# Two-block transformer on one core: the second block's memory keys and values as split passes in pieces, and the test for crowded experts one step earlier

## The chip, the cores and the metric

The kernel runs on one core of a Trainium2 chip. The metric is device time in microseconds from the start of the kernel to its end, median of three executions. One further execution was taken by the hardware profiler, and the rows below come from that one.

## The reference, cut to what matters

Two blocks work on one sequence of 256 tokens with 1024 channels, in fp32. The first block has a convolution layer, a dense feed-forward layer, a layer of sliding-window attention and a layer of eight experts, of which each token takes two. The second block has two hybrid layers, each with a feed-forward layer behind it. Each hybrid layer also attends to a memory of 256 rows, and the keys and values of that memory do not depend on the tokens:

```
def memory_attn(q, mem_n, w_mkv):
    kv = (mem_n @ w_mkv).reshape(B, M, 2, N_HEADS_M, HEAD_DIM)
    s = jnp.einsum('bshd,bmhd->bhsm', q, kv[:, :, 0])
    p = jax.nn.softmax(s, axis=-1)
    o = jnp.einsum('bhsm,bmhd->bshd', p, kv[:, :, 1])
...
def second_block(x, mem, ...):
    for l in range(DEPTH):                     # two layers
        # keys and values of layer l: rms_norm(mem, g_mem[l]) @ w_mkv[l], 1024 x 512
        x = hybrid_layer(x, mem, ...)
    return rms_norm_2(x, norm_final)
...
def moe_swiglu(h, router, we_gate, we_up, we_down):
    top_v, top_i = lax.top_k(h @ router, 2)
    gates = one_hot(top_i) * softmax(top_v)    # 256 x 8
    for e in range(N_EXPERTS):
        out = out + gates[..., e:e + 1] * swiglu(h, we_gate[e], we_up[e], we_down[e])
```

## The kernel before

**The order of the work.** A class `Recorder` takes all operations first and then issues them. `flush` hands what was recorded to `issue`, a list scheduler with its own costs and free places for the buffers: it sets the order of each engine's instructions, and each engine executes its own list in that order. All recorded operations carry the line of the one call in `issue` that emits them, L694 in the rows before. `flush` is called at the test described below and at the end, so no operation moves across the test.

**Weights.** A weight tile is 128 x 1024 fp32 (512 KB) and is loaded on SP's queue into one of 28 `large` buffers. The dense layers use *split passes*: `load` makes two halves of a tile, a high half on ACT and the rest on DVE (by subtraction), in two further `large` buffers; `feed` does the same for the activations; `mm3` issues three matmuls of the type fp32r, high x high, high x low, low x high. In the experts and, before the change, in the second block's memory keys and values the matmuls are plain fp32; a plain fp32 matmul stands in the trace as two records.

**Experts.** `experts` runs 32 steps, four for each expert (31 is the last one's fourth). Step n projects up to 96 gathered tokens (`proj(n)`, 16 tiles of `e_in`, in each expert's fourth step 8), applies the activation (`act`), and then does the down projection of the step before (`down(n-1)`, 8 tiles of `e_down`, in a fourth step 4). When an expert is complete, `scatter` adds its result to the tokens: an evacuation of PSUM on ACT and DVE and matmuls on PE. `prepare(0)` gathers the tokens of the first two experts.

**The test.** `route` also yields the count `most` of the fullest expert. `moe` reads it and passes over the code for more than 96 and more than 192 tokens, which does not run with these inputs:

```
self.nc.flush()
most = self.tc.nc.values_load(self.most[0:1, 0:1], min_val=0, max_val=S)
with ExitStack() as inner:
    for base in range(CAP, S, CAP):
        inner.enter_context(self.tc.If(most > base))
        self.scatter(*self.experts(float(base)))
        self.nc.flush(aside=True)
self.scatter(back, y)
self.nc.release(held)
self.fill(200)
```

All 32 steps stand ahead of the test, the scatter of the last expert behind it. Each engine executes its own branch (line 1327 before).

**The memory.** `mem_second(l)` loads the memory (`mem2T`, four tiles of 256 KB), computes the root mean square (`rstd`, `bcast`), scales it by the gains on ACT, loads `c_mk` and `c_mv` (two tiles each) and makes keys and values, 16 plain fp32 matmuls each. `MEM_AT = 2, 200` puts layer 0 behind `prepare(0)` of the first expert and layer 1 behind the last scatter. `AHEAD = 1` loads and splits the first two tiles of `c_qk`, the first hybrid layer's query and key weights, ahead of the test.

## Time and profile before

| | us |
|---|---|
| median of 3 executions | 2179.4 (2177.43 to 2180.08) |
| the profiled execution | 2182.62 |
| its span, first to last instruction | 2180.8 |
| mean granted TensorE clock | 0.992 |
| PE busy in it | 2141.2 (98%) |
| DVE busy | 965.8 (44%) |
| ACT busy | 734.0 (34%) |

The profiled execution takes 1.8 us more than its span, and 3.2 us more than the median. The page has the busy time of each engine (PE matmuls, PEld weight loads, DVE, ACT, POOL); *windows* give the same for a stretch of time, with the granted clock and the load on the DMA engines; the *timeline* gives the operations in order of time with the idle time before them and what ended it.

### The profile page before, as it was taken

What the parts mean: (1) busy time and instruction counts of PE and PEld (TensorE: products, weight loads), DVE (VectorE), ACT (ScalarE), POOL (GpSimd) and SP (SyncE); (2) the same over time, 40 slices, a digit from 0 to 9 for tenths busy, and PEclk for the clock granted to TensorE, in tenths of its full rate; (3) what the DMA queues carried; (4) which work ended last, traced back from release to release, by engine and by line L of the source; (5) the groups of instructions that cost most, each with busy time, mean ns of one, the idle gap of its engine ahead of it and who ended that gap; (6) DMA issues with size and microseconds to landing.
All of it is one profiled execution on the core that took longest, in us unless ns stands there. A gap on an engine that the chain in (4) does not pass through costs nothing. (4 is left out here: it accounts for less than half of the span.)

```text
span 2180.8 us, 57477 instructions
## 1 busy us (share of the span) xinstructions
PE 2141.2 (98%) x25496; PEld 1688.3 (77%) x25496; DVE 965.8 (44%) x2079; ACT 734.0 (34%) x1315; POOL 0.2 (0%) x4
## 2 busy tenths in 40 slices
PE   8999999999999999999999999899999999999998
PEld 8799997866565656656665656688999998899997
DVE  8975659510112011110302021666675566668553
ACT  8564547310101010010101010555554454655442
POOL 0000000000000000000000000000000000000000
PEclk9999999999999999999999999899999999999998
DMA  7445555489999999999899996653456555345550
GB/s 258 144 147 193 194 192 186 165 315 408 376 365 375 394 398 347 401 367 403 345 395 368 403 368 258 234 177 113 154 174 195 192 174 188 117 132 199 193 182 27
DMA packets 156209, 556.74 MB, mean 255 GB/s; under 512 B 17456, under 2 KB 20144, under 8 KB 155952
## 3 DMA queue, kind: packets, MB, share of 16 engines
q1 hardware_dynamic: 155952, 552.98, 69.3%
q8 instruction: 202, 3.31, 0.6%
q14 instruction: 55, 0.45, 0.1%
HBM read 551.87 MB, written 1.05 MB: 254 GB/s over the span
## 5 line engine op out<-in xcount | busy, mean ns | idle before, releaser
L694 PE MATMUL bank<-large,gen 128*32 128x256 f32 (+2 forms) x16896 | 1061.0, 380 | 0.0
L694 PE MATMUL bank<-gen,large 128*128 128x256 f32 x7468 | 943.3, 287 | 11.8 <-ACT large L694 8.1
L694 PEld LDWEIGHTS bank<-large,gen 128*32 128x32 f32 (+1 forms) x16896 | 656.7, 114 | 376.2 <-issue 6.1
L694 PEld LDWEIGHTS bank<-gen,large 128*128 128x128 f32 x7468 | 915.0, 190 | 29.8 <-issue 9.9
L694 DVE TENSOR_TENSOR large<-large,large 128x1024 fp32r<-128x1024 f32 (+1 forms) x356 | 429.6, 1210 | 129.4 <-PE bank L694 92.5
L694 ACT ACTIVATE gen<-bank 32x256 fp32r<-32x256 f32 (+7 forms) x322 | 124.2, 395 | 925.7 <-PE bank L694 897.8
L694 ACT ACTIVATE large<-large 128x1024 fp32r<-128x1024 f32 (+1 forms) x356 | 364.5, 1045 | 208.8 <-PE bank L694 120.6
L694 DVE SCALAR_TENSOR_TENSOR gen<-bank,small,gen 128x256 f32<-128x256 f32 (+2 forms) x100 | 44.3, 447 | 686.1 <-ACT gen L694 686.1
L694 ACT ACTIVATE gen<-gen 128x512 f32<-128x512 f32 (+3 forms) x149 | 89.6, 614 | 176.6 <-DVE gen L694 175.5
L694 DVE TENSOR_TENSOR gen<-bank,gen 32x256 fp32r<-32x256 f32 (+2 forms) x172 | 85.6, 505 | 138.9 <-ACT gen L694 73.4
L694 PE MATMUL bank<-gen,gen 128*128 128x192 f32 (+5 forms) x672 | 109.3, 341 | 11.8 <-ACT gen L694 7.3
L694 PEld LDWEIGHTS bank<-gen,gen 128*64 128x64 f32 (+3 forms) x672 | 68.3, 175 | 49.4 <-DVE gen L694 17.7
L694 DVE TENSOR_TENSOR gen<-gen,gen 128x512 f32<-128x512 f32 (+3 forms) x129 | 81.1, 637 | 50.2 <-ACT gen L694 48.4
L694 PE MATMUL bank<-ct,gen 128*128 128x128 f32 (+2 forms) x370 | 63.3, 275 | 7.1 <-DVE gen L694 6.8
L694 PEld LDWEIGHTS bank<-ct,gen 128*128 128x128 f32 (+1 forms) x370 | 45.2, 158 | 24.8 <-issue 13.2
L694 ACT ACTIVATE gen<-bank,small 128x256 f32<-128x256 f32 (+2 forms) x75 | 41.0, 569 | 50.5 <-PE bank L694 40.2
L694 DVE TENSOR_TENSOR xT<-xT,bank 128x512 f32<-128x512 f32 x64 | 43.6, 686 | 25.8 <-PE bank L694 24.8
L694 DVE SCALAR_TENSOR_TENSOR gen<-bank,gen 128x256 f32<-128x256 f32 (+1 forms) x66 | 25.4, 428 | 55.1 <-PE bank L694 54.5
L694 DVE SCALAR_TENSOR_TENSOR gen<-gen,pt,gen 128x256 f32<-128x256 f32 x108 | 43.3, 488 | 1.7 <-ACT gen L694 1.7
L694 DVE STREAM_TRANSPOSE gen<-gen 128x256 f32<-128x256 f32 (+1 forms) x96 | 38.7, 408 | 2.8
L694 ACT ACTIVATE gen<-gen,small 128x128 f32<-128x128 f32 x72 | 32.0, 448 | 17.8 <-DVE small L694 17.8
L694 DVE COPY small<-bank 32x1 f32<-32x1 f32 (+1 forms) x97 | 14.8, 152 | 46.6 <-ACT gen L694 44.9
(55 smaller groups left out, 374.2 us busy)
## 6 DMA issues: line engine op xcount, KB each, us to landing
large<-e_in SPq DMA_DIRECT2D x448, 512.0 KB, 6.9
large<-e_down SPq DMA_DIRECT2D x224, 512.0 KB, 6.8
large<-c_up SPq DMA_DIRECT2D x64, 512.0 KB, 4.4
large<-c_dn SPq DMA_DIRECT2D x64, 512.0 KB, 4.7
large<-c_g SPq DMA_DIRECT2D x48, 512.0 KB, 3.9
large<-c_qk SPq DMA_DIRECT2D x24, 512.0 KB, 5.9
large<-cv_gate SPq DMA_DIRECT2D x22, 512.0 KB, 4.5
large<-cv_up SPq DMA_DIRECT2D x22, 512.0 KB, 4.6
```

Source lines behind the costliest of these rows:

```text
L694: op.fn(*[real(x) for x in op.args], **{k: real(x) for k, x in op.kw.items()})
```

## The change

`mem_second` becomes a generator `memories` with four pieces: keys and values of layer 0, then of layer 1. The memory is loaded and its root mean square taken once and held. The matmuls become split passes (`load`, `feed`, `ws`, `n256`). Two pieces are taken inside the sliding-window attention (`other` of `attend` takes one behind each of the first two pairs of heads), one behind `prepare(0)`, one behind the test. `experts` becomes a generator as well and stops ahead of its last step, so that the test now stands ahead of step 31: its 8 tiles of `e_in`, 12 tiles of `e_down`, and the scatter come behind it. The loading ahead (`AHEAD`) is gone. Operations are emitted at L698 of the changed file, the test stands at its L1329.

```diff
 class Recorder
                     if key.start is None:
                         key.start = self.total
-                    key.last = self.total
+                    if key.last is None or key.last < 1 << 60:
+                        key.last = self.total
...
     def release(self, aps):
         for ap in aps:
+            ap.tile.last = self.total
             self.drop(ap.tile, 0.0)
...
     def flush(self, aside=False):
         before = dict(self.free)
+        places = {p: list(p.free) for c in self.kinds.values() for p in c.places}
...
-                    p.free = [v if v is None else min(v, top) for v in p.free]
+                    p.free = places[p]
...
 def swa_layer
-        self.attend(gs, False, ot[:6], sink=lambda g: self.P("sinks", order[g]))
+        self.later = self.memories()
+        self.attend(gs, False, ot[:6], sink=lambda g: self.P("sinks", order[g]), other=islice(self.later, 2))
...
 def moe
-        back, y = self.experts()
-        self.ahead = [self.load(self.a["c0_qk"][0, u]) for u in range(AHEAD)]
-        held = [t for j in self.xn for p in j for t in p] + [self.pos, self.gate, back, y[0], y[2]]
-        self.nc.hold(held)
-        self.nc.hold([t for w in self.ahead for p in w for t in p])
-        self.nc.flush()
+        work = self.experts()
+        held = [t for j in self.xn for p in j for t in p] + [self.pos, self.gate] + next(work)
+        nc.hold(held)
+        nc.flush()
...
-        self.scatter(back, y)
-        self.nc.release(held)
-        self.fill(200)
+        for _ in work:
+            pass
+        nc.release(held)
+        next(self.later)
...
 def experts
         prepare(0)
         if not base:
-            self.fill(2)
+            next(self.later)
         for n, s in enumerate(steps):
-            if not base:
-                self.fill(100 + n)
+            if n == len(steps) - 1 - LAST:
+                e = s[0]
+                yield G[e] + list(B[e]) + [t for k in T for t in T[k]] + [Y[e][0], Y[e][2]]
             act(s, proj(s))
...
-        return down(steps[-1])
+        self.scatter(*down(steps[-1]))
...
-    def mem_second(self, l):
+    def memories(self):
         mT = [self.t([128, 2, S], F32, f"m2T{k}") for k in range(4)]
         self.early(mT, a["mem2T"])
         rc = self.rstd(mT)
         rb = self.bcast(rc)
-        for k in range(KT):
-            x = mT[k // 2][:, k % 2]
-            nc.scalar.activation(x, x, AF.Copy, scale=self.P("memn_g", l * 8 + k))
...
+        nc.hold(mT + [rc, rb])
+        for l in range(2):
+            f = self.feed(mT, "memn_g", l * 8)
+            nc.hold([t for p in f for t in p])
+            kT = self.t([128, 2, S], F32, "m2k")
+            w = self.load(a[f"c{l}_mk"][0])
+            p = self.mm()
+            self.ws(p, w, f)
...
+            yield
+            v = self.t([128, 2, 256], F32, "m2v")
+            w = self.load(a[f"c{l}_mv"])
+            p = self.mm()
+            self.n256(p, f, w)
...
+            yield
...
 def hybrid
-                if self.ahead:
-                    w = self.ahead.pop(0)
-                    self.nat(ps, f, w, 4 * u)
-                    nc.release([t for p in w for t in p])
-                    continue
                 w = self.load(a[f"c{l}_qk"][c, u])
```

**SP's queue at the test.** Before, the list of loads from the last one of the experts over the branch to the first weights of the hybrid layer (`gen` and `large` are buffers, the name behind the arrow is the array in memory; `[waits ...]` are the semaphores that the load waits for on SP):

```order
L694 DMA large_37265<-e_down 128x1024 [waits DMAHW0_49,PE_49]
L1327 UNCONDITIONAL_BRANCH [waits DMAHW0_49,DMAHW1_49,DMAHW2_49,DMAHW3_49,DMAHW4_49,DMAHW5_49,DMAHW6_49,DMAHW7_49] x2
L694 DMA gen_37517<-mem2T 128x512 [waits DVE_49,DMAHW1_49,PE_49,Activation_49]
L694 DMA gen_37523<-mem2T 128x512 [waits DMAHW2_49]
L694 DMA large_37557<-c_mk 128x1024 [waits DMAHW5_49]
L694 DMA large_37587<-c_mv 128x1024 [waits DMAHW7_49,DMAHW0_49]
L694 DMA large_37608<-c_qk 128x1024 [waits DMAHW1_49]
L694 DMA gen_37638<-masks 128x384 [waits DMAHW3_49]
L694 DMA large_37657<-c_qk 128x1024 [waits DMAHW5_49]
```

After the change, the same place of SP's queue:

```order
L698 DMA large_37095<-e_down 128x1024 [waits DMAHW4_49,PE_49]
L1329 UNCONDITIONAL_BRANCH [waits DMAHW0_49,DMAHW1_49,DMAHW2_49,DMAHW3_49,DMAHW4_49,DMAHW5_49,DMAHW6_49,DMAHW7_49] x2
L698 DMA large_37388<-e_in 128x1024 [waits DMAHW3_49,DMAHW2_49,DMAHW4_49,DMAHW1_49,DMAHW5_49,DMAHW0_49,DMAHW6_49,DVE_49,DMAHW7_49,PE_49,Activation_49]
L698 DMA large_37390<-e_in 128x1024 [waits DMAHW4_49,DMAHW2_49,DMAHW7_49,DMAHW0_49,PE_49]
L698 DMA large_37404<-e_down 128x1024 [waits DMAHW5_49]
L698 DMA gen_37428<-masks 128x384 [waits DMAHW1_49]
L698 DMA large_37646<-c_mv 128x1024 [waits DMAHW5_49]
L698 DMA large_37652<-c_mv 128x1024 [waits DMAHW6_49]
L698 DMA large_37658<-c_qk 128x1024 [waits DMAHW7_49]
L698 DMA large_37664<-c_qk 128x1024 [waits DMAHW0_49,PE_49]
L698 DMA large_37710<-c_qk 128x1024 [waits DMAHW2_49,DVE_49]
L698 DMA large_37715<-c_qk 128x1024 [waits DMAHW7_49,DMAHW3_49,DVE_49]
```

Between the branch and the first weights of the hybrid layer there stood the memory, its keys' and its values' weights; now 20 expert tiles (8 of `e_in`, 12 of `e_down`) and the 4 masks stand ahead of `c_mv`, and `c_qk` follows it.

**ACT at the test.** Before, ACT's list from its branch on (`bank` is PSUM; `pt` the table of gains):

```order
L1327 UNCONDITIONAL_BRANCH [waits Activation_49] x2
L694 ACTIVATE gen_37515<-bank_15117 32x256 [waits DVE_49,PE_49,Activation_49]
L694 ACTIVATE gen_37515<-bank_15131 32x256
L694 ACTIVATE gen_37526<-bank_15117 32x256 [waits DVE_49]
L694 ACTIVATE gen_37548<-bank_15131 32x256
L694 ACTIVATE gen_37563<-gen_37517 128x512 [waits DMAHW1_49,PE_49]
L694 ACTIVATE gen_37517<-gen_37517,pt 128x256 [waits Activation_49]
```

After the change (`large_37648<-large_37646` is the high half of a weight tile, so it stands behind that tile's load in SP's list above):

```order
L1329 UNCONDITIONAL_BRANCH [waits Activation_49] x2
L698 ACTIVATE gen_37529<-bank_37434 128x128 [waits PE_49]
L698 ACTIVATE gen_37536<-bank_37439 128x128 [waits DVE_49,PE_49,Activation_49]
L698 ACTIVATE gen_37544<-bank_37444 128x128 [waits PE_49,Activation_49]
L698 ACTIVATE large_37648<-large_37646 128x1024 [waits DMAHW4_49,DMAHW5_49,DMAHW3_49,DMAHW6_49,DMAHW2_49,DMAHW7_49,DMAHW1_49,DMAHW0_49]
L698 ACTIVATE large_37654<-large_37652 128x1024 [waits DMAHW4_49,DMAHW3_49,DMAHW6_49,DMAHW2_49,DMAHW7_49,DMAHW1_49,DMAHW0_49]
L698 ACTIVATE large_37660<-large_37658 128x1024 [waits DMAHW7_49,DMAHW4_49,DMAHW2_49]
L698 ACTIVATE large_37684<-large_37682 128x1024 [waits DMAHW4_49,DMAHW3_49,PE_49]
L698 ACTIVATE large_37719<-large_37710 128x1024 [waits DMAHW6_49,PE_49]
L698 ACTIVATE gen_37760<-bank_15298 32x256 [waits PE_49]
L698 ACTIVATE gen_37760<-bank_15312 32x256 [waits PE_49]
```

Before, the evacuations of the last scatter (`gen<-bank 32x256`, twelve) came first behind the branch, then the memory's squares and gains. Now three evacuations of step 31's projection come first, then ten weight splits (two of `c_mv`, eight of `c_qk`), and the first evacuation of the scatter, `gen_37760<-bank_15298`, stands behind all ten.

**PE in the sliding-window attention.** Before, behind the projection's normalization (`ct` are constants, `gen_4176` the keys):

```order
L694 MATMUL bank_4187<-ct,gen_3935 128x128
L694 MATMUL bank_4198<-ct,gen_2914 128x1 x2
L694 MATMUL bank_4204<-gen_2714,large_4028 128x256 [waits DMAHW3_49,DMAHW0_49]
L694 MATMUL bank_4217<-gen_4176,gen_4196 128x128 [waits Activation_49]
L694 MATMUL bank_4224<-gen_4176,gen_4196 128x128
L694 MATMUL bank_4217<-gen_4176,gen_4196 128x256
L694 MATMUL bank_4224<-gen_4176,gen_4196 128x256
L694 MATMUL bank_4241<-ct,gen_4150 128x128 [waits DVE_49,PE_49]
L694 MATMUL bank_4245<-gen_4176,gen_4196 128x128 [waits PE_49]
```

After the change (`large_3869` and `large_3961` are the halves of a tile of layer 0's `c_mk`, `bank_4202` its result; `gen_4200` holds the keys):

```order
L698 MATMUL bank_4202<-gen_4094,large_3869 128x256 [waits Activation_49]
L698 MATMUL bank_4202<-gen_4104,large_3869 128x256
L698 MATMUL bank_4202<-gen_4094,large_3961 128x256
L698 MATMUL bank_4202<-gen_1342,large_3882 128x256
L698 MATMUL bank_4202<-gen_1411,large_3882 128x256
L698 MATMUL bank_4291<-gen_4200,gen_4265 128x128 [waits Activation_49]
L698 MATMUL bank_4298<-gen_4200,gen_4265 128x128
L698 MATMUL bank_4291<-gen_4200,gen_4265 128x256
L698 MATMUL bank_4298<-gen_4200,gen_4265 128x256
L698 MATMUL bank_4312<-ct,gen_4171 128x128 [waits DVE_49,PE_49]
L698 MATMUL bank_4202<-gen_1342,large_3991 128x256
```

Before, the first matmul of layer 0's keys (`bank_4204`) stood among the attention's, and most came in the routing and just ahead of the first expert's; now the 96 split matmuls of layer 0's keys and values stand among the attention's matmuls, and those of layer 1's keys come in the routing.

## Rows read from the trace of the kernel before

**Rows 1.** The page's first part: busy time, share of span and instructions of each engine.
```profile
PE 2141.2 (98%) x25496; PEld 1688.3 (77%) x25496; DVE 965.8 (44%) x2079; ACT 734.0 (34%) x1315; POOL 0.2 (0%) x4
```

**Rows 2.** Windows: busy time, granted clock, DMA share, GB/s; expert end to hybrid start.
```profile
core 0: us, PE busy (x) PEld busy (x) DVE busy (x) ACT busy (x) POOL busy (x), PEclk, DMA share, GB/s
1345.00:1371.20 26.20, 26.19 (x484) 15.48 (x476) 4.02 (x8) 2.73 (x5) 0.00 (x0) 1.00 0.02 5
1371.20:1376.20 5.00, 0.51 (x2) 0.31 (x3) 1.24 (x3) 1.70 (x5) 0.00 (x0) 1.00 0.26 71
1376.20:1393.40 17.20, 14.52 (x40) 10.89 (x41) 15.07 (x38) 15.98 (x35) 0.00 (x0) 0.50 0.99 359
1393.40:1403.60 10.20, 10.20 (x51) 9.01 (x50) 9.43 (x14) 5.02 (x7) 0.00 (x0) 1.00 0.92 361
```

**Rows 3.** The test's instructions, line 1327: count, ns min/median/max, first and last start in us.
```profile
L1327 SPq COMPARE_BRANCH  x1: 50/50/50, 1340.5 to 1340.5; - x1
L1327 PEldq COMPARE_BRANCH  x1: 3682/3682/3682, 1370.1 to 1370.1; - x1
```

**Rows 4.** Timeline around the test: start, duration, engine, operation, [idle before <-releaser].
```profile
1334.76 36.43 PE L694 MATMUL bank<-large,gen 128*32 128x256 f32 x668
1336.26 4.21 SPq L694 DMA_DIRECT2D large<-c_qk  x2
...
1373.94 2.53 SPq L694 DMA_DIRECT2D gen<-mem2T  x4
1373.95 1.16 ACT L694 ACTIVATE gen<-bank 32x256 fp32r<-32x256 f32 x3 [15.74 <-PEq L1327]
...
1385.53 3.30 ACT L694 ACTIVATE gen<-xT,pt 128x256 fp32r<-128x256 f32 x8
1387.10 1.67 DVE L694 SCALAR_TENSOR_TENSOR gen<-xT,pt,gen 128x256 fp32r<-128x256 f32 x4
...
1390.82 2.94 ACT L694 ACTIVATE large<-large 128x1024 fp32r<-128x1024 f32 x3
...
1394.78 1.06 ACT L694 ACTIVATE large<-large 128x1024 fp32r<-128x1024 f32 x1 [1.03 <-DMA large<-c_qk]
...
1397.11 2.19 ACT L694 ACTIVATE large<-large 128x1024 fp32r<-128x1024 f32 x2 [1.27 <-DMA large<-c_qk]
```

**Rows 5.** Timeline of PE: layer 1's memory values, a broadcast, first `c_qk` matmuls.
```profile
1395.90 4.48 PE L694 MATMUL bank<-large,gen 128*128 128x256 f32 x20
1400.22 0.59 PE L694 MATMUL bank<-gen,ct 128*128 128x256 f32 x2
...
1403.60 5.58 PE L694 MATMUL bank<-large,gen 128*128 128x512 f32 x23
```

**Rows 6.** Windows of the sliding-window attention, and one of a feed-forward layer's split matmuls.
```profile
365.00:372.00 7.00, 6.13 (x47) 4.03 (x45) 6.99 (x58) 6.33 (x19) 0.00 (x0) 1.00 0.75 301
372.00:399.00 27.00, 26.94 (x163) 15.80 (x163) 20.97 (x114) 23.52 (x87) 0.00 (x0) 1.00 0.01 2
1700.00:1750.00 50.00, 50.00 (x424) 50.00 (x423) 27.51 (x30) 23.21 (x26) 0.00 (x0) 1.00 0.56 186
```

**Rows 7.** Timeline of PE in the routing: layer 0's memory keys, first and last piece.
```profile
427.95 1.89 PE L694 MATMUL bank<-gen,large 128*128 128x256 f32 x8
...
437.10 2.84 PE L694 MATMUL bank<-gen,large 128*128 128x256 f32 x12
```

**Rows 8.** The page's part on groups: the two halves of a weight split.
```profile
L694 DVE TENSOR_TENSOR large<-large,large 128x1024 fp32r<-128x1024 f32 (+1 forms) x356 | 429.6, 1210 | 129.4 <-PE bank L694 92.5
L694 ACT ACTIVATE large<-large 128x1024 fp32r<-128x1024 f32 (+1 forms) x356 | 364.5, 1045 | 208.8 <-PE bank L694 120.6
```

**Rows 9.** One tile's view: from issue to landing of `c_qm`, which is loaded alone.
```profile
DMA to landing us min/median/max: 3.5/3.7/3.8
```

**Rows 10.** Windows: the DMA's fastest stretch; PE's first work behind its wait at 1601.
```profile
1200.00:1250.00 50.00, 50.00 (x936) 30.09 (x929) 4.15 (x12) 1.99 (x6) 0.00 (x0) 1.00 1.02 403
1605.00:1608.30 3.30, 3.30 (x17) 3.30 (x17) 2.80 (x5) 2.62 (x4) 0.00 (x0) 0.50 0.03 7
```

More of the change, by code (lines that the diff above doesn't have):

```diff
@@ L3 @@
 from contextlib import ExitStack
+from itertools import islice
 import numpy as np
@@ L40 @@
 EARLY = 6
-AHEAD = 1
 LOAD_SHIFT = 0
@@ L47 @@
 GATES = 2
+LAST = 0
 MEM_BIAS = (0, 0)
@@ L1122, in conv_layer @@
             self.attend(self.mem_heads(qT, self.mkT, self.mv), True, mo)
-        self.fill(0)
         pm = self.mm("pm")[:, :S]
@@ L1228, in swa_layer @@
             self.attend(self.mem_heads(mT, self.mkT, self.mv), True, ot[6:])
-        self.fill(1)
         bias = {}
@@ L1317, in moe @@
     def moe(self):
+        nc = self.nc
         self.route()
-        back, y = self.experts()
-        self.ahead = [self.load(self.a["c0_qk"][0, u]) for u in range(AHEAD)]
-        held = [t for j in self.xn for p in j for t in p] + [self.pos, self.gate, back, y[0], y[2]]
-        self.nc.hold(held)
-        self.nc.hold([t for w in self.ahead for p in w for t in p])
-        self.nc.flush()
+        work = self.experts()
+        held = [t for j in self.xn for p in j for t in p] + [self.pos, self.gate] + next(work)
+        nc.hold(held)
+        nc.flush()
         most = self.tc.nc.values_load(self.most[0:1, 0:1], min_val=0, max_val=S)
@@ L1329, in moe @@
                 inner.enter_context(self.tc.If(most > base))
-                self.scatter(*self.experts(float(base)))
-                self.nc.flush(aside=True)
-        self.scatter(back, y)
-        self.nc.release(held)
-        self.fill(200)
+                for _ in self.experts(float(base)):
+                    pass
+                nc.flush(aside=True)
+        for _ in work:
+            pass
+        nc.release(held)
+        next(self.later)
     def onehot(self, e, base):
@@ L1476, in experts @@
                 prepare(s[0] + 1)
-        return down(steps[-1])
-    def fill(self, at):
-        for l in range(2):
-            if MEM_AT[l] == at:
-                self.nc.shift = MEM_BIAS[l]
-                self.mem_second(l)
-                self.nc.shift = 0
-    def mem_second(self, l):
+        self.scatter(*down(steps[-1]))
+    def memories(self):
         nc, a = self.nc, self.a
@@ L1492, in mem_second @@
         rb = self.bcast(rc)
-        for k in range(KT):
-            x = mT[k // 2][:, k % 2]
-            nc.scalar.activation(x, x, AF.Copy, scale=self.P("memn_g", l * 8 + k))
-        kT = self.t([128, 2, S], F32, "m2k")
-        v = self.t([128, 2, 256], F32, "m2v")
-        w = self.load_raw(a[f"c{l}_mk"][0])
-        p = self.mm()
-        for i in range(2):
-            for k in range(KT):
-                nc.tensor.matmul(p[:, i * S:(i + 1) * S], w[i][:, k], mT[k // 2][:, k % 2], start=k == 0, stop=k == KT - 1)
-        nc.vector.tensor_tensor(kT, p.rearrange("p (a s) -> p a s", a=2), rb[:, None, :].to_broadcast([128, 2, S]),
-                                op=OP.mult)
-        w = self.load_raw(a[f"c{l}_mv"])
-        p = self.mm()
-        for k in range(KT):
-            for j in range(2):
-                nc.tensor.matmul(p[:, j * 256:(j + 1) * 256], mT[k // 2][:, k % 2, j * 128:(j + 1) * 128],
-                                 w[k // 4][:, k % 4], start=k == 0 and j == 0, stop=k == KT - 1,
-                                 skip_group_check=True)
-        for j in range(2):
-            nc.scalar.activation(v[:, j], p[:, j * 256:(j + 1) * 256], AF.Copy, scale=rc[:, j:j + 1])
-        nc.hold([kT, v])
-        self.m2[l] = (kT, [v[:, j] for j in range(2)])
+        nc.hold(mT + [rc, rb])
[6 more added lines that the diff above has]
+            self.ws(p, w, f)
+            nc.vector.tensor_tensor(kT, p.rearrange("p (a s) -> p a s", a=2), rb[:, None, :].to_broadcast([128, 2, S]),
+                                    op=OP.mult)
+            nc.hold([kT])
+            yield
[3 more added lines that the diff above has]
+            self.n256(p, f, w)
+            for j in range(2):
+                nc.scalar.activation(v[:, j], p[:, j * 256:(j + 1) * 256], AF.Copy, scale=rc[:, j:j + 1])
+            nc.hold([v])
+            nc.release([t for p in f for t in p])
+            self.m2[l] = (kT, [v[:, j] for j in range(2)])
+            if l:
+                nc.release(mT + [rc, rb])
+            yield
     def hybrid(self, l):
```

## The prediction

> **What bounds the kernel now.** The busy times come first: PE works in 2141 of 2181 us, DVE and ACT in under half [rows 1]. So the time is PE's work plus the few places at which PE waits or runs at a lower clock. The change touches two such stretches: the attention with the routing and the first expert behind it, and the test. I read the windows next, because they show both. Up to 1371.2 PE is dense with expert matmuls and the DMA engines are idle; then PE works 0.5 us of 5; then it runs 17.2 us at a granted clock of 0.50, the lower of its two levels (1.2 and 2.4 GHz), while ACT and DVE are busy for 16 and 15 of them with the second memory; then 10.2 us at full clock until the first `c_qk` matmul [rows 2]. The test's own rows say why: SP passed its branch at 1340.5, but PE's branch starts at 1370.1 and takes 3.7 us [rows 3], and the first load behind the test issues at 1373.94, as ACT's first instruction does [rows 4]. So the loads behind the test start 2.75 us after PE's last matmul ahead of it (1334.76 + 36.43 = 1371.19 to 1373.94).
>
> Where the DMA engines are fastest they move 403 GB/s for 50 us [rows 10]; the sum below goes by that. The Trainium skill ("DMA: Bandwidth & Descriptors", section "Where 436 GB/s comes from") has HBM bind loads at some 358 GB/s per core; by that figure the 31.5 tiles of 512 KB that are counted below would take 46.1 us instead of 41.0. The trace goes beyond it.
>
> **The change, part one: attention to first expert (A).** Layer 0's keys and values were 32 plain matmuls, 64 records; 20 records start in 1400.22 - 1395.90 = 4.32 us [rows 5], 0.216 each, so 13.8 us. Now layer 0's keys and values and layer 1's keys are 48 matmuls of three passes, 144 records; 424 such records take 50 us [rows 6], 0.118 each, so 17.0 us. PE has 3.2 us more to do. It has nowhere to hide it: of the 34 us of the attention PE is idle 0.93 (7.00 - 6.13 and 27.00 - 26.94) [rows 6]. The pieces in the routing that covered its waits, 8 records to 12 [rows 7], are replaced there by those of layer 1's keys.
>
> By the rows three passes cost 3 x 0.118 / (2 x 0.216) = 0.82 of a plain matmul [rows 5, 6]. The Trainium skill ("FP8 and Floating Point Precision", section "TensorE Precision Notes") counts true FP32 as four passes through the array; by that three would cost 3/4, 48 x 0.324 = 15.6 us, and PE's work would grow by 1.7 instead of 3.2.
>
> ACT and DVE get more too. In the attention they are busy 29.85 and 27.96 of 34 us [rows 6]. Added there are 16 halves of activations (ACT 3.30 / 8 = 0.41 each, DVE 1.67 / 4 = 0.42, [rows 4]; two layers' feeds) and six weight splits (1.05 and 1.21, [rows 8]): some 12.9 and 14.0 us. With PE's 96 records (11.3 us) the stretch grows to 45 us, and ACT needs 43 of them. Engines so full in a chain of normalization, exponentials and transposes wait for one another; before shows no such stretch with split passes in it. From below the wait costs nothing and PE's idle 0.9 us is filled too; from above I take the overlap of one third of the added ACT and DVE work as lost, 5 us. I choose 1.5, nearer to nothing, because PE has matmuls without such waits to fill with. A = 3.2 + 1.5 = **+4.7** (2.3 to 8.2).
>
> **Part two: the test (B).** The stretch to compare runs from the start of the last 20 expert tiles' matmuls to the first `c_qk` matmul. 240 matmuls are 480 records, 26.0 us by the row of 484 in 26.2 [rows 2]. Before, they start at 1371.2 - 26.0 = 1345.2, and the first `c_qk` matmul at 1403.6 [rows 5]: 58.4 us. Now this stretch begins with the test, and none of its 20 tiles can be loaded before it.
>
> - 2.75 us until the first load [rows 4]. This wait does not vanish: the first `e_in` load waits for PE, and behind it stands SP's whole list.
> - Then the loads in SP's order: 20 expert tiles, four masks (1.5 tiles' worth), two of `c_mv`, eight of `c_qk`: 31.5 tiles. These count to the eighth tile of `c_qk`, because ACT, which takes its list in order, has ten splits of these ten weight tiles in front of the scatter's first evacuation. From below, 524 KB at 403 GB/s is 1.30 us each [rows 10], and the first lands 3.7 us after issue [rows 9]: 41.0 + 2.4 = 43.4 us. From above, by what the loads behind the test took before: from 1373.94 to the split at 1397.11, which waited for the fifth `c_qk` tile behind the test (three, one, and this one; two had come ahead of it at 1336.26) [rows 4], there landed 2 + 4 + 1.5 + 5 = 12.5 tiles in 23.1 us, 4.4 more than 16.3 + 2.4. That makes 47.8. I take the middle, 45.6: the loads before waited partly for buffers, and 27 buffers for 31 tiles will make some wait too.
> - The last split, 1.05 on ACT [rows 8]. PE has its 20 tiles done long before that: 2.75 + 3.7 + 26.0, plus half of the 3.3 us at 0.50 with which PE came back from a wait elsewhere [rows 10], is 34 us, against 49.4. Then eight matmuls of layer 1's values follow, and PE stands before the scatter.
> - The scatter: three evacuations on ACT, 1.2 us [rows 4], then 16 scatter matmuls and the other 40 of layer 1's values on PE, 56 x 0.118 = 6.6 at full clock or 13.2 at half. After the wait before the clock was at half for 17.2 us [rows 2]; after the other for 3.3. So 7.8 to 14.4; I take the middle, 11.1.
>
> Sum 2.75 + 45.6 + 1.05 + 11.1 = 60.5, **B = +2.1** (-3.4 to +7.6). So the second memory's 17.2 us with its load, its root mean square and its gains do leave the path, but the ten splits put the DMA's time for 31.5 tiles on it. What comes behind the first `c_qk` matmul stands on PE in the order of before; the tiles that are loaded earlier give nothing back there, as PE is dense.
>
> A + B = +6.8. The profiled execution, span 2180.8 and 1.8 around it, would go from 2182.6 to 2189.4; the median of before lies 3.2 below its profile, so I predict 2179.4 + 6.8 = **2186.2 us**.
>
> **Rivals.**
> - *No change.* The DMA moves 403 GB/s to the end, the clock is back at once, the attention hides the splits: A = 3.2, B = -3.4, 2179.2 us. For it speaks that 403 held for 50 us; against it that the window behind the test showed 359 and 361 [rows 2].
> - *Heavier.* The loads lose 4.4 us as before, the clock stays at half, the attention loses 5: A = 8.2, B = 7.6, 2195.2 us. For it speaks the same window; against it that the 4.4 us belong partly to buffers that other work held.
> - *Faster: ACT does not hold the scatter.* If the loads of `c_mv` and `c_qk` land as fast as PE works through the 20 tiles, PE alone sets the stretch: 2.75 + 3.7 + 26.0 + 1.7 + 7.8 = 42.0, B = -16.4, and with A 2167.7 us. It decides once the tenth weight tile has landed within 34 us of the start, that is when the list of 31.5 tiles needs under 31 us. At 403 GB/s it needs 43, so this would take loads that start ahead of PE's branch; SP passed the branch 33 us ahead of PE, but its next load waited for PE [rows 3, 4].
> - *The change doesn't do what it says:* the order shows it done; no chance of its own.
>
> **How the numbers follow.** 0.2% of 2179.4 is 4.4 us, about what a measurement of this kernel can tell from no change: faster is below 2175.0, slower above 2183.8. The forecast's case, up to 2190, has 0.42; no change 0.25; heavier 0.20; faster 0.13. So slower 0.42 + 0.20 = 0.62. The likeliest case alone spans 2183.8 to 2190. The range reaches from 2176.5, which holds nearly all of the no-change case, to 2194.5, near the sum of the upper bounds; left out are the faster case and the tip of the heavier.
>
> **What would show it.** Right: ACT's first `gen<-bank 32x256` behind the test is idle until a `large<-c_qk` load and comes over 10 us after the last expert matmul; PE waits that long on ACT at the first scatter, with its clock at half beside it; PE stands idle 6 to 7 us from its last matmul ahead of the test to the first expert matmul behind it; the first expert begins 3 to 6 us later; from the test's step to the first `c_qk` matmul lie 57 to 64 us. Wrong: a scatter that starts straight after the last expert matmul (then B is near -16); an expert start that is no later (A at nothing); or a first `e_in` load that issues at SP's branch, long ahead of PE's.

## The result, and the profile after

The changed kernel takes 2191.1 us (median of five, 2189.1 to 2192.7), before 2179.4 (median of five on the same chip): a ratio of 1.0051, 95% interval 1.0036 to 1.0066. It is slower by 11.7 us; the forecast was 6.8.

The page's busy times of after, to be read against [rows 1]:

```profile
span 2190.2 us, 57707 instructions
PE 2134.4 (97%) x25554; PEld 1682.7 (77%) x25554; DVE 976.5 (45%) x2085; ACT 740.0 (34%) x1318; POOL 0.2 (0%) x4
```

PE is busy 6.8 us less than before in a span that is 9.4 us longer. So what was added is waiting and time at the lower clock, not work. PE's waits for ACT in the whole of after (engine, line, who is waited for: us in total, times, longest):

```profile
PE bank L698 <- ACT gen L698: 16.4, 10, 12.7
```

**The test (B).** The timeline of after from the test to the first `c_qk` matmul, which answers to [rows 4, 5]:

```profile
1317.74 34.27 PE L698 MATMUL bank<-large,gen 128*32 128x256 f32 x628
...
1354.74 6.28 SPq L698 DMA_DIRECT2D large<-e_in  x8
...
1358.87 2.79 PE L698 MATMUL bank<-large,gen 128*32 128x256 f32 x24 [6.86 <-DMA large<-e_in]
...
1404.85 1.06 ACT L698 ACTIVATE large<-large 128x1024 fp32r<-128x1024 f32 x1 [2.05 <-DMA large<-c_qk]
1405.81 1.14 ACT L698 ACTIVATE gen<-bank 32x256 fp32r<-32x256 f32 x3
...
1407.00 0.58 PE L698 MATMUL bank<-gen,gen 96*128 96x256 f32 x1 [12.72 <-ACT gen L698]
...
1417.44 6.86 PE L698 MATMUL bank<-large,gen 128*128 128x512 f32 x29
```

PE's last matmul ahead of the test ends at 1317.74 + 34.27 = 1352.0. From there 2.7 us pass until the first load, 50.1 until ACT's last weight split starts, 1.0 in that split, and 11.6 with the scatter until the first `c_qk` matmul: 65.4 us, against 58.4 before. B is +7.0. The same stretch, seen as windows with the columns of [rows 2]:

```profile
1362.00:1388.20 26.20, 25.65 (x456) 13.95 (x456) 1.65 (x6) 0.83 (x3) 0.00 (x0) 0.98 1.03 407
...
1391.20:1394.30 3.10, 2.40 (x8) 1.81 (x8) 2.67 (x3) 2.22 (x3) 0.00 (x0) 0.50 0.74 280
1394.30:1407.00 12.70, 0.00 (x0) 0.00 (x1) 9.32 (x8) 8.30 (x10) 0.00 (x0) 0.50 0.84 278
1407.00:1414.30 7.30, 7.30 (x30) 6.74 (x31) 5.71 (x14) 5.59 (x15) 0.00 (x0) 0.50 0.71 246
1414.30:1417.40 3.10, 3.10 (x28) 3.10 (x28) 3.03 (x7) 2.95 (x7) 0.00 (x0) 1.00 0.48 169
```

PE has done its 20 tiles at 1388.2, after 36 us. Then it does eight matmuls and stands for 12.7 us, with the clock at its lower level (1.2 GHz) until 1414.3. The DMA engines move 407 GB/s while PE works, and 278 to 280 from 1391.2 to 1407.0, while ACT and DVE make the halves. SP's timeline shows the `c_qk` loads in three groups there; between them SP issues nothing for 5.6 and 3.4 us:

```profile
1385.26 2.69 SPq L698 DMA_DIRECT2D large<-c_qk  x4
...
1393.58 0.80 SPq L698 DMA_DIRECT2D large<-c_qk  x2
...
1397.78 7.11 SPq L698 DMA_DIRECT2D large<-c_qk  x6
```

SP's waits between 1380 and 1406 name DVE first, that is, buffers that DVE had to free. Smaller ones are for loads that had not landed; the longest of those is 3.1 us for `c_mv`, in the first of the two gaps.

```profile
SPq L698 <- DVE large L698: 9.4, 6, 2.5
```

**The attention (A).** Three places on PE bound it: the last projection matmul of the attention layer, the first routing matmul (`128*8`), the first expert matmul (`128*32`). Before:

```profile
351.77 11.70 PE L694 MATMUL bank<-large,gen 128*128 128x512 f32 x50
...
420.72 1.89 PE L694 MATMUL bank<-gen,pt 128*8 128x256 f32 x8
...
446.77 0.64 PE L694 MATMUL bank<-large,gen 128*32 128x256 f32 x8
```

After, with three rows from the attention between them:

```profile
351.80 9.93 PE L698 MATMUL bank<-large,gen 128*128 128x512 f32 x42
...
363.02 1.66 PE L698 MATMUL bank<-gen,large 128*128 128x256 f32 x12
...
383.26 1.10 PE L698 MATMUL bank<-large,gen 128*128 128x256 f32 x7
...
389.64 0.70 PE L698 MATMUL bank<-ct,gen 128*128 128x128 f32 x3 [1.82 <-DVE gen L698]
...
435.18 1.89 PE L698 MATMUL bank<-gen,pt 128*8 128x256 f32 x8
...
453.56 1.72 PE L698 MATMUL bank<-large,gen 128*32 128x256 f32 x28
```

From the end of the projections (363.47 and 361.73) to the routing it takes 57.3 before and 73.5 after: +16.2. Of these, 96 new records of 0.118 are 11.3; four plain records that stood there before take off 0.9, and a broadcast for the memory's root mean square that came in adds 0.4. The remaining 5.3 is called the loss: time beyond PE's new work. From the routing to the first expert it takes 26.1 and 18.4: -7.7, where the other 60 plain records and the broadcast went (13.4) and 48 split ones came (5.7), so nothing is lost there. A is +8.5. (A second execution of each has its first expert at 446.26 and 454.68, +8.4.) The expectations below count the loss as 4.9, without the four records and the broadcast. It has a place. All 96 memory matmuls run between 363.0 and 384.1, the start of the attention, where before PE had attention matmuls to do. Windows of after behind it [rows 6]:

```profile
372.00:384.00 12.00, 12.00 (x88) 9.39 (x87) 9.49 (x34) 8.09 (x27) 0.00 (x0) 1.00 0.36 132
384.00:390.00 6.00, 4.18 (x42) 3.33 (x41) 5.48 (x32) 5.77 (x20) 0.00 (x0) 1.00 0.70 255
390.00:400.00 10.00, 10.00 (x29) 4.44 (x29) 6.26 (x36) 5.75 (x23) 0.00 (x0) 0.51 0.02 7
400.00:412.00 12.00, 12.00 (x82) 8.20 (x81) 8.99 (x35) 10.21 (x38) 0.00 (x0) 0.98 0.00 1
```

When the filling is used up, PE waits 1.8 us in the 6 before 390, and the next 10 us go by at a clock of 0.51, which is nearly all at the lower level: about 5 us of PE's time.

A + B = 15.5, more than the 11.7 of the medians. One matmul of the first hybrid layer, the 128x128 at 1471.3 in the profile of before, stands at 1485.4 in that of after, 14.1 later. Below, this matmul is called the mark. The 15.5 become 14.1 mainly because PE came to the attention 1.7 us earlier in the profile of after: before ran some 3.4 us at the lower clock just ahead of 100 us (window below), after had 1.00 there.

```profile
96.00:100.00 4.00, 4.00 (x7) 1.60 (x6) 4.00 (x43) 3.40 (x4) 0.00 (x0) 0.57 0.72 218
```

From the mark to the end of the span the profile of before takes 709.5 us, that of after 704.8. A part is a stall at 1601 [rows 10] that a second execution of before doesn't have; but that one still takes 707.4, and all other kernels take 703.6 to 706.2. So the changed kernels get back some 2 us behind the mark. Which stretch gives them is open. Spans differ by 9.4 with the first execution of before and 13.8 with the second.

### The profile page after: what moved, and what is told of

Read it like the earlier page. It is cut to its first block, busy times and chain, and to the rows that moved or that the text cites. A ratio compares the mean times of both kernels' runs of the same rounds, so it can differ in the third digit from the quotient of the medians.

```text
span 2190.2 us, 57707 instructions
## 1 busy us (share of the span) xinstructions
PE 2134.4 (97%) x25554; PEld 1682.7 (77%) x25554; DVE 976.5 (45%) x2085; ACT 740.0 (34%) x1318; POOL 0.2 (0%) x4
## 3 DMA queue, kind: packets, MB, share of 16 engines
q1 hardware_dynamic: 155376, 551.94, 69.3%
HBM read 550.82 MB, written 1.05 MB: 252 GB/s over the span
## 5 line engine op out<-in xcount | busy, mean ns | idle before, releaser
L698 PE MATMUL bank<-large,gen 128*32 128x256 f32 (+2 forms) x16528 | 1051.2, 380 | 11.4 <-DMA large<-e_in 7.2
L698 PE MATMUL bank<-gen,large 128*128 128x256 f32 x7488 | 935.1, 285 | 10.5 <-ACT large L698 8.0
L698 PEld LDWEIGHTS bank<-large,gen 128*32 128x32 f32 (+1 forms) x16528 | 645.4, 114 | 381.7 <-issue 15.1
L698 PEld LDWEIGHTS bank<-gen,large 128*128 128x128 f32 x7488 | 909.4, 189 | 26.8 <-issue 9.9
L698 DVE TENSOR_TENSOR large<-large,large 128x1024 fp32r<-128x1024 f32 (+1 forms) x364 | 438.6, 1210 | 148.3 <-PE bank L698 90.8
L698 ACT ACTIVATE large<-large 128x1024 fp32r<-128x1024 f32 (+1 forms) x364 | 373.7, 1045 | 258.0 <-PE bank L698 108.1
L698 ACT ACTIVATE gen<-bank 32x256 fp32r<-32x256 f32 (+6 forms) x315 | 121.5, 396 | 923.4 <-PE bank L698 912.2
L698 DVE SCALAR_TENSOR_TENSOR gen<-bank,small,gen 128x256 f32<-128x256 f32 (+2 forms) x100 | 44.3, 446 | 687.8 <-ACT gen L698 687.8
L698 ACT ACTIVATE gen<-gen 128x512 f32<-128x512 f32 (+3 forms) x145 | 86.9, 611 | 157.0 <-DVE gen L698 155.9
L698 DVE TENSOR_TENSOR gen<-bank,gen 32x256 fp32r<-32x256 f32 (+2 forms) x166 | 83.1, 508 | 125.7 <-PE bank L698 65.1
L698 PE MATMUL bank<-gen,gen 128*128 128x192 f32 (+5 forms) x668 | 110.0, 345 | 17.3 <-ACT gen L698 14.4
L698 PEld LDWEIGHTS bank<-gen,gen 64*128 64x128 f32 (+3 forms) x668 | 68.3, 177 | 53.3 <-ACT gen L698 22.6
L698 DVE TENSOR_TENSOR gen<-gen,gen 128x512 f32<-128x512 f32 (+3 forms) x126 | 79.2, 636 | 51.8 <-ACT gen L698 50.1
L698 PE MATMUL bank<-ct,gen 128*128 128x128 f32 (+2 forms) x366 | 63.1, 277 | 8.0 <-DVE gen L698 8.0
L698 PEld LDWEIGHTS bank<-ct,gen 128*128 128x128 f32 (+1 forms) x366 | 44.2, 156 | 25.2 <-issue 12.6
L698 DVE TENSOR_TENSOR xT<-xT,bank 128x512 f32<-128x512 f32 x64 | 43.5, 686 | 24.2 <-PE bank L698 23.3
L698 ACT ACTIVATE gen<-bank,small 128x256 f32<-128x256 f32 (+2 forms) x75 | 41.0, 569 | 30.2 <-PE bank L698 23.2
L698 DVE SCALAR_TENSOR_TENSOR gen<-bank,gen 128x256 f32<-128x256 f32 (+1 forms) x66 | 25.4, 427 | 54.7 <-PE bank L698 54.1
L698 DVE SCALAR_TENSOR_TENSOR gen<-gen,pt,gen 128x256 f32<-128x256 f32 (+1 forms) x120 | 49.0, 485 | 1.7 <-ACT gen L698 1.7
L698 PE MATMUL bank<-large,large 128*32 128x256 f32 (+1 forms) x416 | 38.1, 374 | 0.0
L698 ACT ACTIVATE gen<-gen,small 128x128 f32<-128x128 f32 x72 | 31.9, 444 | 17.8 <-DVE small L698 17.7
L698 DVE STREAM_TRANSPOSE gen<-gen 128x256 f32<-128x256 f32 (+1 forms) x90 | 36.0, 406 | 2.6
```

Source lines behind the costliest of these rows:

```text
L698: op.fn(*[real(x) for x in op.args], **{k: real(x) for k, x in op.kw.items()})
```

## The experiments

The ratio is to before on the same chip, with its 95% interval. "Attention" is the time from the start of the last projection matmul to the first routing matmul, "prelude" from there to the first expert matmul, "wait" PE's longest wait for ACT behind the last expert tile.

| kernel | median us (before there) | ratio, 95% | attention | prelude | wait | mark |
|---|---|---|---|---|---|---|
| before | 2179.4 | 1 | 57.6 | 26.1 | 4.0 | 1471.3 |
| changed | 2191.1 (2179.4) | 1.0051, 1.0036 to 1.0066 | 73.9 | 18.4 | 12.7 | 1485.4 |
| e1 | 2181.5 (2177.0) | 1.002, 1.001 to 1.003 | 74.5 | 18.4 | 4.3 | 1475.5 |
| e2 | 2190.4 (2177.0) | 1.0072, 1.0058 to 1.0085 | 66.4 | 24.4 | 10.1 | 1481.9 |
| e3 | 2203.5 (2177.0) | 1.0122, 1.0106 to 1.0137 | 57.6 | 26.1 | 12.7 | 1496.9 |
| e4 | 2189.4 (2177.0) | 1.0062, 1.0048 to 1.0076 | 73.9 | 18.4 | 10.5 | 1483.6 |
| e5 | 2188.0 (2177.5) | 1.0045, 1.0032 to 1.0058 | 74.4 | 18.3 | 10.8 | 1483.5 |
| e6 | 2175.1 (2177.5) | 0.9984, 0.9972 to 0.9996 | 77.2 | 18.4 | 3.7 | 1473.0 |
| e7 | 2187.0 (2177.5) | 1.0038, 1.0027 to 1.005 | 57.6 | 26.1 | 1.1 | 1476.1 |
| e8 | 2178.1, one run (2177.5) | - | 57.6 | 26.1 | 4.0 | 1469.0 |
| e9 | 2186.6 (2178.4) | 1.004, 1.0026 to 1.0053 | 70.7 | 18.3 | 12.6 | 1482.6 |
| e10 | 2191.7 (2178.4) | 1.0061, 1.0047 to 1.0075 | 74.1 | 18.4 | 12.9 | 1486.8 |
| e11 | 2173.6 (2178.4) | 0.9981, 0.9972 to 0.999 | 69.3 | 18.3 | 4.0 | 1467.6 |

### e1: the scatter ahead of the splits

With a flush behind the last expert step the scheduler has to place that step and its scatter before it sees any later operation. Nothing else differs.

```diff
         for _ in work:
             pass
+        nc.flush()
         nc.release(held)
```

> The changed kernel with one more flush behind the last expert's scatter, so that the scheduler issues step 31 and its scatter before it sees the second memory's last piece and the hybrid layer. On ACT three evacuations of the scatter then follow step 31's, and only the two c_mv and two c_qk splits stand among the other nine. Theory (ACT's ten splits hold the scatter): PE's wait of 12.7 us at the scatter falls under 3, the first c_qk matmul comes 14 to 18 us earlier than in the changed kernel (1417.4), and the time is 2174 to 2180, a part of it lost again at 1601. Rival (the loads of c_qk set the time, whatever stands ahead on ACT): PE waits for c_qk instead, and the time is within 4 us of the changed kernel, 2187 to 2191.

Measured: 2181.5, and the mark 10 us ahead of that of after. The timeline of e1 shows ACT's first evacuations straight behind the last expert matmul, and weight splits still among the later ones:

```profile
1388.56 1.16 ACT L698 ACTIVATE gen<-bank 32x256 fp32r<-32x256 f32 x3 [14.77 <-PE bank L698]
...
1389.77 0.38 PE L698 MATMUL bank<-gen,gen 96*128 96x256 f32 x1 [0.85 <-ACT gen L698]
...
1395.21 1.06 ACT L698 ACTIVATE large<-large 128x1024 fp32r<-128x1024 f32 x1
...
1396.29 1.57 ACT L698 ACTIVATE gen<-bank 32x256 fp32r<-32x256 f32 x4
...
1396.72 1.78 PE L698 MATMUL bank<-gen,gen 96*128 96x256 f32 x5 [4.30 <-ACT gen L698]
```

So ACT's splits did hold the scatter: 10 us of the delay at the mark are theirs, 7 by the medians (11.7 over before, now 4.6), or 9 against the second measurement of the changed kernel (e10, 13.3 over). The median is 1.5 above what the theory gave. Four splits of 1.05 us still stand among the scatter's evacuations, and PE waits 4.3 us between the scatter's matmuls for ACT, where the theory had under 3. That removing these four too would gain the rest was not tried. The first `c_qk` matmul comes 19 us earlier than in after (1398.4), but most of the others follow only at 1414.0, so the mark is the better measure.

### e2: layer 0's keys and values behind the routing

```diff
-        self.attend(gs, False, ot[:6], sink=lambda g: self.P("sinks", order[g]), other=islice(self.later, 2))
+        self.attend(gs, False, ot[:6], sink=lambda g: self.P("sinks", order[g]))
...
-            next(self.later)
+            for _ in range(3):
+                next(self.later)
```

> The changed kernel without the two pieces inside the attention: layer 0's keys and values and layer 1's keys are all recorded behind prepare(0). The scheduler still puts layer 0's keys among the attention's matmuls, but the values (48 records, two weight splits) and layer 1's keys come in the routing; the place of the test is as in the changed kernel. Theory (the 4.9 us by which the attention grew beyond its new matmuls are a wait for DVE, loaded with the new splits, and the half clock behind it): with less on DVE and ACT in the attention the wait and the half clock go, and the time is 2185 to 2188. Rival (the split passes cost that wherever they stand): no change, 2189 to 2193.

Measured: no gain, as the rival had it; against before the ratio is not below that of after. A window of e2 in the place of the half clock, and one of its whole attention:

```profile
390.00:395.00 5.00, 5.00 (x25) 2.52 (x24) 4.57 (x26) 4.57 (x21) 0.00 (x0) 1.00 0.00 2
...
363.65:430.02 66.37, 63.03 (x450) 49.47 (x449) 47.48 (x213) 39.50 (x120) 0.00 (x0) 1.00 0.40 142
```

The clock is whole, but attention and prelude together take 90.8 us, against 92.3 in after and 83.7 before. The passes that left the attention came back in the prelude. In the attention PE now stands idle for 3.3 us (66.37 - 63.03), against 2.4 in after and 0.9 before, so waits took the place of the half clock in part. Only 1.5 us of the loss is got back. Layer 0's keys still stand among the attention's matmuls here, so this doesn't show what moving all the pieces out would give.

### e3: the new place of the test with the old memory code

The rest of the edit puts `mem_second` back as it was. The loading ahead (`AHEAD`) stays out, as in the changed kernel.

```diff
-        next(self.later)
+        self.fill(200)
...
-            next(self.later)
+            self.fill(2)
```

> The new place of the test with the memory as before (plain fp32, layer 0 behind prepare(0), layer 1 behind the test). ACT has ten splits ahead of the scatter here too, and 35.5 tiles' worth of loads (20 expert tiles, the memory, four for keys and values, masks, eight of c_qk). Theory (the test's place costs by the loads and by ACT's order, the memory's pieces by the attention, and the two add up): the expert start is that of before, the first c_qk matmul comes some 12 us later than before, and the time is 2185 to 2192. Rival (the loss comes from the memory's split passes, the test's place costs nothing): 2176 to 2181.

Measured: 26.6 us slower than before, worse than either reading foresaw. The attention is that of before, so all of it lies at the test. The timeline of e3:

```profile
1381.15 1.23 ACT L698 ACTIVATE gen<-gen 128x512 f32<-128x512 f32 x2 [42.87 <-DMA gen<-mem2T]
...
1386.51 0.57 ACT L698 ACTIVATE gen<-bank 128x128 f32<-128x128 f32 x3
...
1387.55 2.79 PE L698 MATMUL bank<-large,gen 128*32 128x256 f32 x24 [9.01 <-DVE gen L698]
...
1409.73 0.58 PE L698 MATMUL bank<-gen,gen 96*128 96x256 f32 x1 [12.71 <-ACT gen L698]
```

ACT stands for the memory's load, whose squares are in its list ahead of the expert's evacuation, and PE's last tiles wait 9.0 us behind that; then the splits hold the scatter for 12.7. The new place of the test lets whatever comes later stand ahead of the last expert step on ACT.

### e4: the old place of the test with the new memory code

```diff
-        work = self.experts()
+        back, y = self.experts()
+        self.ahead = [self.load(self.a["c0_qk"][0, u]) for u in range(AHEAD)]
...
-        for _ in work:
-            pass
+        self.scatter(back, y)
         nc.release(held)
         next(self.later)
```

> The memory's split passes in pieces as in the changed kernel, the test and the two tiles of c_qk ahead of it as before. Nine splits stand ahead of the scatter on ACT, with nine tiles to load behind the test: 2.75 + 9 x 1.3 + 2.4 + 1.05 = 18 us, then 8 to 14 to the first c_qk matmul, against 32.4 before. Theory (the two parts add up): +6.8 in attention and routing, 0 to -6 at the test, 2180 to 2187. Rival (the whole loss comes with the split passes, the test's place is harmless): 2189 to 2193.

Measured: 12.4 us slower than before. That is past what the theory gave and is the rival's number, but not for the rival's reason: e3 shows that the test's place is not harmless, and e6 below that most of e4's loss is not the split passes themselves. ACT holds the scatter at the old place too, with nine splits. The timeline of e4:

```profile
1400.22 0.58 PE L699 MATMUL bank<-gen,gen 96*128 96x256 f32 x1 [10.47 <-ACT gen L699]
```

### e5: layer 0 plain in the attention

```diff
...
-            w = self.load(a[f"c{l}_mk"][0])
+            w = self.load(a[f"c{l}_mk"][0]) if l else self.load_raw(a[f"c{l}_mk"][0])
             p = self.mm()
-            self.ws(p, w, f)
+            if l:
+                self.ws(p, w, f)
+            else:
+                for i in range(2):
+                    for k in range(KT):
+                        nc.tensor.matmul(p[:, i * S:(i + 1) * S], w[i][:, k], f[k // 2][:, k % 2], start=k == 0, stop=k == KT - 1)
...
```

> The changed kernel, but layer 0's keys and values in plain fp32 (64 records of 0.216 us, no halves on ACT and DVE, only eight scalings on ACT) at their new place in the attention; layer 1's pieces and the test as changed. Theory (the attention's growth beyond its new matmuls, 4.9 us, comes from the halves on ACT and DVE): the attention grows by 13.8 us and at most 1 more, without half clock in it, the first expert begins 1 to 3 us earlier than in the changed kernel, and the time is 1 to 3 us below it. Rival (any matmuls among the attention's delay its chain as much): the attention grows by 17 to 19 us, and the time is 1 to 3 us above the changed kernel.

Measured: the attention takes 16.8 us more than before, 13.8 for the plain passes and 3.0 of loss, where split passes lost 4.9 (in the count of the expectation). Neither reading had this. The windows at the place show the half clock again, though layer 0's halves on ACT and DVE aren't there:

```profile
394.00:400.00 6.00, 6.00 (x21) 3.05 (x22) 4.48 (x26) 4.24 (x17) 0.00 (x0) 0.53 0.00 1
400.00:402.00 2.00, 2.00 (x14) 1.19 (x12) 1.18 (x6) 1.75 (x9) 0.00 (x0) 0.71 0.00 0
```

The wait ahead of it is 1.84 us, as long as in after (1.82). By these clocks the lower level lasted some 7 us here and some 10 in after, which is 1.7 us of PE's time and nearly all of the 1.9 by which the losses differ. So no part of the loss is shown to be due to these halves, on which the prediction put it.

### e6: e4 with the scatter ahead of the splits

```diff
         self.scatter(back, y)
+        nc.flush()
         nc.release(held)
```

> The kernel of e4 (new memory, test and loading ahead as before) with a flush behind the scatter, so that the scatter's evacuations come first on ACT. Theory (ACT's splits held the scatter there too): PE's wait of 10.9 us for ACT goes, the first c_qk matmul comes 9 to 13 us earlier than in e4 (1415.7), and the time falls by as much, to 2176 to 2181. Rival (behind the test PE has too little work to cover the loads of c_mv and c_qk, so a wait for these takes its place): under 5 us gained, 2184 to 2190.

Measured: 14.3 us less than e4 and, with a ratio of 0.9984, less than before. The new memory code thus wins at the test more than it loses in the attention: the first expert of e6 begins at 457.7, 11.5 us later than in e8, its mark stands only 4.0 later. The timeline of e6 has the scatter behind the last expert tile:

```profile
1384.55 1.16 ACT L699 ACTIVATE gen<-bank 32x256 fp32r<-32x256 f32 x3 [15.65 <-PEq L1332]
...
1385.76 0.58 PE L699 MATMUL bank<-gen,gen 96*128 96x256 f32 x1 [3.67 <-ACT gen L699]
```

Its attention took 77.2 us in the profiled execution, e4's 73.9, with the same code there and the same wait of 1.82 us. The half clock behind that wait lasted 17 us in e6 and some 10 in e4, which makes up the 3 us:

```profile
392.00:409.00 17.00, 17.00 (x52) 8.72 (x52) 9.99 (x49) 8.81 (x34) 0.00 (x0) 0.50 0.03 9
```

### e7: e3 with the scatter ahead of the splits

```diff
...
         for _ in work:
             pass
+        nc.flush()
         nc.release(held)
-        next(self.later)
+        self.fill(200)
```

> The kernel of e3 (new test, old memory) with a flush behind the scatter. Theory (both of PE's waits in e3, 9.4 us among the last expert tiles and 13.1 ahead of the scatter, come from ACT's order, which had the second memory's squares and ten splits in front): both fall under 3 us, and the time falls by 15 to 22, to 2181 to 2189. Rival (the loads of the second memory and of the 20 tiles set the time): less than 8 us gained, above 2195.

Measured: 16.5 us less than e3. Both waits of e3 are gone, as ACT's list has the last expert step and the scatter first. What is left, 9.5 us over before with an attention and a prelude as before, is the price of the test's new place together with the loading ahead that the change dropped. No run separates these two.

### e8 and e10: the two kernels again

> The kernel before, unchanged, for a second profile. Theory (the stall of 3.5 us at 1601, which no changed kernel shows, belongs to that one execution): no such stall, and a span of 2174 to 2178. Rival (it belongs to the order of before): the stall is there again, and the span is 2179 to 2182.

Measured: before, looked at again, has a wait of 1.1 us at 1601 in place of 3.2, no half clock behind it, and a span of 2176.4; its timeline there:

```profile
1601.13 3.37 PE L694 MATMUL bank<-gen,large 128*128 128x256 f32 x26 [1.10 <-ACT gen L694]
```

> The changed kernel again, on the chip of e9, for a second profile and a comparison on one chip. Theory (7 us in attention to experts and 7 at the test): 2188 to 2192, with the wait near 389 and the half clock behind it, and PE's wait of about 13 us for ACT ahead of the scatter. Rival (one of the two belongs to the one execution): it is missing here.

Measured: 13.3 us over before on this chip, and both waits come again; the timeline of e10:

```profile
390.72 0.70 PE L698 MATMUL bank<-ct,gen 128*128 128x128 f32 x3 [1.82 <-DVE gen L698]
...
1407.72 0.58 PE L698 MATMUL bank<-gen,gen 96*128 96x256 f32 x1 [12.92 <-ACT gen L698]
```

### e9: the pieces later in the attention

```diff
-        self.attend(gs, False, ot[:6], sink=lambda g: self.P("sinks", order[g]), other=islice(self.later, 2))
+        self.attend(gs, False, ot[:6], sink=lambda g: self.P("sinks", order[g]), other=chain((None,) * 3, islice(self.later, 2)))
```

> The changed kernel with the two pieces of layer 0 taken behind the fourth and fifth pair of heads instead of the first and second, so that PE's 96 split matmuls stand farther back among the attention's. Nothing else differs. Theory (in the changed kernel PE takes all 96 between 363.0 and 384.1, ahead of the attention's chain, which then lies open with nothing to fill it: the wait at 387 and the half clock to 400): the wait behind them and the half clock go, the attention grows by 10 to 13 us instead of 16.2, the first expert begins 3 to 6 us earlier, and the time falls by as much below the changed kernel (e10, on the same chip). Rival (the halves on ACT and DVE are the cause, wherever they stand among the heads): no change within 2 us.

Measured: 5.1 us less than e10 beside it. The attention takes 3.4 less than in e10 (13.1 more than before), and the windows show most of the half clock gone:

```profile
390.00:400.00 10.00, 9.25 (x69) 6.67 (x68) 9.72 (x35) 7.13 (x23) 0.00 (x0) 1.00 0.63 195
400.00:412.00 12.00, 11.49 (x61) 7.87 (x61) 7.66 (x30) 8.40 (x29) 0.00 (x0) 0.86 0.16 59
```

The wait is still there, but shorter: the timeline has 1.25 us where after had 1.82. (At the test its first wait was shorter too, 3.0 and 1.7 us in two parts instead of 6.7 in e10: only seven `e_in` loads stand behind the test there, and PE begins with a tile straight behind its branch. So some 2 of the 5.1 are not the attention's.)

### e11: old place of the test, scatter first, pieces late

The edits of e4, e6 and e9 together.

> The kernel of e6 (test and loading ahead as before, scatter first) with the late pieces of e9. Theory (the two repairs add up): 3 to 6 us below e6 (2175.1), 2169 to 2173, the fastest of all. Rival (the late pieces push the halves into the routing or the experts' start, and what is won in the attention is lost there): 2174 to 2177.

Measured: 2173.6 us, ratio 0.9981 (0.9972 to 0.999), 4.8 us ahead of before, between the theory and the rival. It has the lowest median, but its interval lies over that of e6 (0.9972 to 0.9996), so the two can't be told apart. The gains add up at most in part: late pieces were worth 5.1 us to the changed kernel, and here, against e6, 1.5 by the medians and 2.4 by the distances to before.

## Why the prediction was right, and where its sizes were off

- **The direction and both mechanisms held.** Each sign that was named is there: ACT's first `gen<-bank 32x256` behind a `c_qk` split, 17.6 us after PE's last expert matmul (1388.2 to 1405.8); PE's 12.7 us wait for ACT with the half clock beside it; 6.86 us idle at the test; first expert later. Two sizes lie outside what was named: the first expert came 6.8 us later (453.56 against 446.77; the profile of after had come to the attention 1.7 earlier), not 3 to 6, and the stretch from the test to `c_qk` took 65.4 us, not 57 to 64.
- **That the time lies near the forecast is in part luck.** A measured 8.5, past its upper bound of 8.2, and B 7.0 of at most 7.6. By its parts this is the rival "heavier": the loads lost time, the clock stayed at half for most of the scatter, the attention lost 5 us, and the sum of 15.5 is nearly that rival's 15.8. The medians differ by 11.7 only, because the changed kernels get back some 2 us behind the mark, where the prediction had nothing; the rest is within what single executions differ by (2189.1 to 2192.7 for the changed kernel).
- **A: the passes were right, the wait was mis-sized.** The price of the passes held where nothing else disturbs it: from the routing to the first expert it gives -7.7, as measured. The wait was put at 1.5, with 5 as the bound ("one third of the added ACT and DVE work", which is 4.3 to 4.7), and measured 5.3. The step that failed is the choice "nearer to nothing, because PE has matmuls without such waits to fill with": PE filled with them at once, so none were left when the softmax work came, and the clock fell on top. e9, where they come later, gets 3.4 back in that stretch, and the median falls by 5.1 beside e10, of which some 2 belong to the test; this shows the place as a cause. The prediction put the wait on full ACT and DVE. In e5, without layer 0's halves, the same wait comes (1.84 us), and the loss is smaller only by what a shorter half clock gives; so their share isn't shown.
- **B: the loads were mis-sized.** Of its four terms three held: 2.75 measured 2.73, the last split 1.0, the tail 11.1 measured 11.6. The loads were put at 45.6, between 43.4 and 47.8, and took 50.1. The DMA held 407 GB/s for the expert tiles, then fell to 278 to 280 while SP stood. That DVE's splits held the buffers is read from SP's waits, which also name loads under way; no run with more buffers was made, so this cause is not shown by experiment. The Trainium skill ("DMA: Bandwidth & Descriptors", section "Where 436 GB/s comes from") has HBM as the bound of loads at some 358 GB/s; the trace is over it (407) while the expert tiles are loaded, and under it (278 to 280) while SP stands between the `c_qk` loads.
- **The rival "faster" was rightly put aside, but its price was wrong.** It gave B = -16.4, 23 below the measured B, if ACT doesn't hold the scatter because the loads come early. e1 loosens the hold by the order on ACT instead, and the mark moves by 10: four splits among the evacuations and a 4.3 us wait inside the scatter remain, and the half clock too.
- **The change is two edits of opposite worth.** With ACT freed in each, the new memory code at the old place is at 0.9984 (e6), the new place with the old memory at 1.0038 (e7), both new at 1.002 (e1). So the memory code gains some 3.5 to 3.9 us (1 - 0.9984, and 1.0038 - 1.002; each ratio is known to about 2.6 us), and the place of the test, with the loading ahead gone, costs 8 even then (1.002 - 0.9984, and 1.0038 - 1); the ten splits ahead of the scatter cost another 7 to 10.

## What to carry to other kernels

When work behind a barrier has loads and conversions of its own, look on each engine's list for what it puts ahead of the next step's evacuation: here ten weight splits, cheap in themselves, made a scatter wait for the last of 31.5 tiles on a queue. One line that puts the scatter's first evacuations ahead was worth 7, 15 and 17 us in the three kernels that had it added (changed to e1, e4 to e6, e3 to e7, by the distances to before). Work that is meant to fill another stretch's waits must stand where these waits are; given at the start it is used up before they come.

## What the runs showed of the hardware that was not expected

- A short wait among small matmuls can cost more than itself: after 1.8 us of waiting the granted clock of after was 0.51 for 10 us. The other four profiled executions with that attention (e1, e4, e6, e10) have the same wait, and the half clock came behind it each time, for some 10 us in three and 17 in e6. In e9 a wait of 1.25 us was followed by 0.86 over 12 us, and in e11, after the same wait, by 1.00. What decides between these was not settled. The window of e11:

```profile
400.00:412.00 12.00, 10.74 (x69) 7.03 (x66) 8.87 (x36) 8.84 (x31) 0.00 (x0) 1.00 0.41 133
```

and the wait in its timeline:

```profile
401.72 0.70 PE L699 MATMUL bank<-ct,gen 128*128 128x128 f32 x3 [1.25 <-DVE gen L699]
```

- The DMA engines moved 411 GB/s over 20 us while PE was busy throughout at a granted clock of 0.97, more than the 403 of [rows 10]:

```profile
1362.00:1382.00 20.00, 20.00 (x360) 10.91 (x360) 1.65 (x6) 0.83 (x3) 0.00 (x0) 0.97 1.03 411
```
